# Seven products for sixteen instead of eight row chunks of each down projection

## The chip, the cores and the metric

One core of one Trainium2 chip runs the whole kernel. The metric is the device time of one launch in microseconds, the median of several runs.

## The reference, cut to what matters

A two-layer decoder trunk over 512 tokens of width 1024. Each layer has a gated feed-forward block, a mixer (attention and retention) and a second gated feed-forward block, each followed by a residual sum and a layer norm, so four feed-forward blocks run in all.

```python
D_MODEL = 1024; SEQ = 512; DEPTH = 2
D_FF = ((8 * D_MODEL // 3 + 127) // 128) * 128      # 2816, 22 chunks of 128

def swiglu_ffn(x, w_gu, w_down):
    a, u = jnp.split(x @ w_gu, 2, axis=-1)
    return (jax.nn.silu(a) * u) @ w_down

for l in range(DEPTH):
    x = layer_norm(DEEPNORM_ALPHA * x + 0.5 * swiglu_ffn(x, ffn1_w_gu[l], ffn1_w_down[l]), ...)
    x = layer_norm(DEEPNORM_ALPHA * x + hybrid_mixer(x, ...), ...)
    x = layer_norm(DEEPNORM_ALPHA * x + 0.5 * swiglu_ffn(x, ffn2_w_gu[l], ffn2_w_down[l]), ...)
```

The change is in the last matrix product of `swiglu_ffn`: a (512 x 2816) matrix of gated values times a (2816 x 1024) weight.

## The kernel before

**Every product in three matmuls.** All data are fp32. `split` (line 158) writes an operand as a rounded part on ScalarE (line 159, a cast) and a rest on VectorE (line 160, a subtraction that needs the cast). `mm3` (line 165) then issues three matmuls: high by high (line 168), high by low (169), low by high (170).

**Weights.** `Weights.pump` (line 50) walks a list of items, one for each unit of 128 x 1024 split weights, in the order in which TensorE uses them. There are six buffers for split units (`UBUFS`), and `W.done` frees one and starts the split of a later item into it. Raw weights come by SyncE's queue in pieces of 1 MB into two buffers (tag `raw`); the loads are started by `pump` ahead of their use.

**The gated half.** `ffn` (line 475) works through eleven pairs of chunks, the last nine by a seven-product scheme of their own (`glu7`), and leaves the gated values in `hT`: 22 chunks of 128 rows, 512 tokens wide. Its weight sums stand in two buffers of tag `S`.

**The down half.** Here `acc` is all eight PSUM banks: four blocks of 128 tokens (`t`) by two halves of 512 columns (`q`). Of the 22 chunks the first eight are taken as a 2 x 2 block product: `hT` is cut in two halves of four chunks and two halves of 256 tokens, the weight in two halves of 512 rows and two of 512 columns. Seven block products (`seventh`, line 680) replace eight. Each has two steps (`g`), and each step has 12 matmuls of 128 x 512 into two banks of one column half: `low`, `high`, `left`, `right` (lines 707 and 708). The other fourteen chunks take 24 matmuls each, into all eight banks (`chunk`, line 698; the last four, `TAIL`, by token block so that the norm of one block runs beside the next).

- Three of the seven products use weight blocks as they are (`p1`, `p2`, `p3` in `down_items`, line 340). The other four use sums of blocks, which are made in two SBUF tiles `R[0]` and `R[1]` (the two `S` buffers; each has two halves, `x` 0 and 1): SyncE loads a first block (line 356), and GpSimd adds others by accumulating DMAs (`add`, line 349). A sum that has been split may be added to again, for a later product (the third argument of `cut`).
- The token side needs sums too: `fifth` (three VectorE subtractions, lines 647 to 649) and `third` (one, line 655); the others are plain splits (`operand`, `whole`). A generator, `operands`, makes them three steps ahead, in four buffers.
- After some products `into` (line 710) adds the two banks to, or takes them from, the residual `Y` on VectorE (line 714). The next product that accumulates in those banks cannot write a bank until it has been read.

The order of the products before is: 1 `p1` into `low`, 2 sum into `high`, 3 `p2` into `left`, 4 sum into `low`, 5 `p3` into `right`, 6 sum into `low`, one plain chunk, 7 sum into `low`. Y is updated after 1, 2, 4 and 6. The order of instructions on each engine's queue is fixed when the program is built, by a list scheduler that follows program order and its own durations; each engine then runs its queue strictly in that order.

Of the kernel before, what the change touches and what calls it, by code (L numbers as in the profile page):

```python
# [7 lines left out]
F32 = mybir.dt.float32  # L8
F32R = mybir.dt.float32r
AF = mybir.ActivationFunctionType  # L10
ALU = mybir.AluOpType
# [7 lines left out]
P = 128  # L19
# [7 lines left out]
GN_EPS = 1e-6  # L27
SCALE = HD ** -0.5
TAIL = 4
SEVEN = (2, 3, 4, 5, 6, 7, 8, 9, 10)  # L30
UBUFS = 6
LOOK = 6
# [60 lines left out]
class Trunk:  # L93
# [230 lines left out]
    def ffn_items(self, gu, down, key):  # L324
        items = []
        for fp in range(NFP):
            a = self.cols_item(gu, fp * 256, (key, "a", fp))
            u = self.cols_item(gu, DFF + fp * 256, (key, "u", fp))
            if fp == 0:
                items += [a[0], u[0], a[1], u[1]]  # L330
            else:
                items += self.seven_items(a, u) if fp in SEVEN else a + u
        rows = []
        for fp in range(4, NFP):
            late = [self.tail_units if fp * 2 + c >= NF - TAIL else None for c in range(2)]
            rows += self.rows_item(down, fp * 256, (key, "d", fp), late)
        R = {}
        return items + self.down_items(down, key, R, rows[0]) + rows[1:]

    def down_items(self, w, key, R, row):  # L340

        def block(i, j, g):
            r0 = i * 512 + g * 256
            return w[r0 : r0 + 256, j * 512 : (j + 1) * 512].rearrange("(k p) c -> p k c", p=P)

        def add(g, x, i, j):
            self.tc.keep_in_program_order(self.nc.gpsimd.dma_start(R[g][:, x], block(i, j, g), accum_op=ALU.add))
# [22 lines left out]
        p1, p2, p3 = (self.wide_item(w, j * 512, i, (key, "b", i, j)) for i, j in ((0, 0), (1, 0), (1, 1)))  # L372
# [102 lines left out]
    def ffn(self, g_, b, out=None):  # L475
        nc, tc, W = self.nc, self.tc, self.W
        with ExitStack() as ctx:
# [99 lines left out]
            for fp in range(NFP):  # L577
                if fp == 0:
                    us = [W.get() for _ in range(6)]
                    self.pin = False  # L580
                    au = [us[0:2], us[2:4]]
                    self.finish(self.pend[:2])
                    more = []
                    for t0 in (0, 256):
                        for c in range(2):
                            glu(au[c], c, t0, t0 + 256)
                            if t0:
                                W.done(2)
# [41 lines left out]

            def part(g, i, j):

                return hT[:, j * 4 + 2 * g : j * 4 + 2 * g + 2, i * 256 : (i + 1) * 256]

            def operand(src):
                hh, hl = (v.rearrange("p (f t) -> p f t", f=2) for v in pair())
# [5 lines left out]
            def fifth(g):  # L642

                a11, a21, a22 = part(g, 0, 0), part(g, 1, 0), part(g, 1, 1)
                hh, hl = (v.rearrange("p (f t) -> p f t", f=2) for v in pair())
                s1 = self.s1[:, g]
                nc.vector.tensor_sub(s1, a21, a22)
# [13 lines left out]
                return hh, hl  # L661

            def operands():
                for g in range(2):
                    yield fifth(g)
                for g in range(2):
                    yield operand(part(g, 0, 1))
                for g in range(2):
                    yield operand(part(g, 0, 0))
                for g in range(2):  # L670
                    yield third(g)
                for g in range(2):
                    yield operand(part(g, 1, 0))
                yield whole(8)
                for g in range(2):
                    yield operand(part(g, 1, 1))
                for f in range(9, NF):
                    yield whole(f)

            def seventh(banks, u, h, new):  # L680

                for f in range(2):
                    for i, b_ in enumerate(banks):
                        ts = slice(i * P, (i + 1) * P)
                        self.mm3(b_, (h[0][:, f, ts], h[1][:, f, ts]), (u[0][:, f, :], u[1][:, f, :]),
                                 new and f == 0, False, skip_group_check=True)
                self.step()
# [25 lines left out]
                    y = self.Y[:, t0 + i, q * 512 : (q + 1) * 512]  # L713
                    nc.vector.scalar_tensor_tensor(out=y, in0=y, scalar=scale, in1=b_, op0=ALU.mult, op1=sign)

            for n, (banks, new, more) in enumerate((
                    (low, True, (0, 0, ALPHA)), (high, True, (0, 1, ALPHA)), (left, True, None),
                    (low, False, (0, 1, 1.0, ALU.subtract)), (right, True, None),
                    (low, False, (2, 1, ALPHA, ALU.subtract)), (low, False, None))):
                if n == 6:  # L720
                    chunk(8)
                for g in range(2):
                    u, h = W.get(), ahead.pop(0)
                    ahead.append(next(split))
                    seventh(banks, u, h, new and g == 0)
                    W.done(2 if n == 0 and g == 1 else 1)
                if more:
                    into(banks, *more)
# [400 lines left out]
```

## Time and profile before

| | |
|---|---|
| median of 3 runs | 1821.43 us (1821.35 to 1822.49) |
| the profiled execution: time / span | 1826.58 us / 1824.8 us |
| TensorE busy | 1800.6 us, 12074 matmuls |
| VectorE busy | 1339.8 us |
| ScalarE busy | 878.7 us |
| granted TensorE clock, mean | 0.995 |
| the down halves begin at | 234, 792, 1135 and 1695 us |

"Busy" counts overlapping pipelined matmuls once. PEclk is the granted TensorE clock as a share of full speed. In a timeline a row shows start, duration, engine, line, operation, output and inputs, count, and in brackets the idle time of the engine before it and what ended it. PE is TensorE, DVE VectorE, ACT ScalarE, POOL GpSimd, SP SyncE.

### The profile page before, as it was taken

The page shows a single profiled execution, that of the slowest core. Times are in us where ns is not written, and L with a number is a line of the kernel's source. Part 1 is how long each engine was busy: PE and PEld are TensorE (multiplying, and loading weights), DVE is VectorE, ACT ScalarE, POOL GpSimd, SP SyncE. Part 2 cuts the span into 40 slices and gives each one's busy share as a digit, 9 for nine tenths or more (in the row PEclk, how much of TensorE's full clock was granted, in tenths as well). Part 3 has the DMA queues.
Part 4 walks back from the last instruction along what each step waited for, and adds up shares of the span by engine and source line. Part 5 has one row for each costly group of instructions (what it writes and reads, how often), then busy time and mean ns, then how long its engine had stood idle before and what let it go on. Part 6 is the DMA issues. An engine that isn't in the chain of part 4 may idle for free.

```text
span 1824.8 us, 29291 instructions
## 1 busy us (share of the span) xinstructions
PE 1800.6 (99%) x12074; PEld 1632.9 (89%) x12074; DVE 1339.8 (73%) x1942; ACT 878.7 (48%) x1439; POOL 123.8 (7%) x104
## 2 busy tenths in 40 slices
PE   9999999999999999999999999999999999999998
PEld 9999978887789999988899999788877899999786
DVE  7888784656768788876678886847567687887845
ACT  4455553278723455554235554532785234555530
POOL 0000010111110000020000001001011100000101
PEclk9999999999999999999999999999999999999999
DMA  5233485223122332484222236641233122334731
GB/s 185 93 125 107 144 203 162 64 82 89 51 93 70 110 99 93 137 210 168 86 70 93 93 106 190 172 157 42 83 91 93 46 93 93 107 125 130 198 111 47
DMA packets 151990, 205.87 MB, mean 113 GB/s; under 512 B 4656, under 2 KB 116016, under 8 KB 151856
## 3 DMA queue, kind: packets, MB, share of 16 engines
q1 hardware_dynamic: 143152, 187.23, 31.5%
q0 software_dynamic: 8704, 16.78, 5.3%
q8 instruction: 94, 1.54, 0.4%
q14 instruction: 40, 0.33, 0.1%
HBM read 201.89 MB, written 2.10 MB: 112 GB/s over the span
## 4 chain that ended last, share of the span: by engine, by line
PE 82%; issue 7%; DVE 5%; ACT 3%; DMA 2%; POOL 1%; SPq 0%; POOLq 0%; DVEq 0%; ACTq 0%
PE ps L170 27%; PE ps L169 26%; PE ps L168 26%; DMA R<-in_ffn_w_down_dram 1%; ACT sw L898 1%; POOL sw L900 1%; PE ps L428 1%; DMA raw<-in_ffn_w_gu_dram 1%; DVE ul L160 1%; DVE Y L464 1%; ACT uh L159 1%; DVE st L454 1%; DVE Y L461 0%; PE ps L1008 0%; DVE Y L452 0%
## 5 line engine op out<-in xcount | busy, mean ns | idle before, releaser
L168 PE MATMUL ps<-xh,uh 128*128 128x256 f32 (+1 forms) x1616 | 482.1, 298 | 0.0
L170 PE MATMUL ps<-xh,ul 128*128 128x256 f32 (+1 forms) x1616 | 479.1, 297 | 0.4 <-DVE ul L160 0.4
L169 PE MATMUL ps<-xl,uh 128*128 128x256 f32 (+1 forms) x1616 | 478.8, 296 | 0.4 <-DVE xl L160 0.4
L160 DVE TENSOR_TENSOR ul<-raw,uh 128x1024 fp32r<-128x1024 f32 (+1 forms) x325 | 336.6, 1049 | 77.9 <-ACT uh L159 77.2
L159 ACT CAST uh<-raw 128x1024 fp32r<-128x1024 f32 (+1 forms) x325 | 291.4, 913 | 202.9 <-PE ps L169 127.6
L168 PE MATMUL ps<-Th,uh 128*128 128x256 f32 x1152 | 319.3, 277 | 0.7 <-DVE Q L547 0.7
L169 PE MATMUL ps<-Tl,uh 128*128 128x256 f32 x1152 | 318.7, 277 | 0.0
L170 PE MATMUL ps<-Th,ul 128*128 128x256 f32 x1152 | 318.3, 276 | 0.0
L168 PEld LDWEIGHTS ps<-xh,uh 128*128 128x128 f32 x1616 | 307.9, 191 | 10.2 <-issue 1.6
L170 PEld LDWEIGHTS ps<-xh,ul 128*128 128x128 f32 x1616 | 307.9, 191 | 9.3 <-DVE ul L160 0.8
L169 PEld LDWEIGHTS ps<-xl,uh 128*128 128x128 f32 x1616 | 308.0, 191 | 8.6 <-DVE xl L160 0.8
L170 PE MATMUL ps<-uh,hl 128*128 128x512 f32 x640 | 255.0, 398 | 4.0 <-DVE hl L160 4.0
L168 PE MATMUL ps<-uh,hh 128*128 128x512 f32 x640 | 253.4, 396 | 4.7 <-ACT hh L159 4.7
L169 PE MATMUL ps<-ul,hh 128*128 128x512 f32 x640 | 253.6, 396 | 0.0
L159 ACT CAST uh<-S 128x1024 fp32r<-128x1024 f32 x144 | 151.2, 1050 | 153.1 <-PE ps L169 148.2
L160 DVE TENSOR_TENSOR ul<-S,uh 128x1024 fp32r<-128x1024 f32 x144 | 175.9, 1222 | 62.1 <-ACT uh L159 61.4
L168 PEld LDWEIGHTS ps<-Th,uh 128*128 128x128 f32 x1152 | 216.7, 188 | 0.9 <-DVE Q L547 0.9
L169 PEld LDWEIGHTS ps<-Tl,uh 128*128 128x128 f32 x1152 | 216.7, 188 | 0.0
L170 PEld LDWEIGHTS ps<-Th,ul 128*128 128x128 f32 x1152 | 216.4, 188 | 0.0
L168 PEld LDWEIGHTS ps<-uh,hh 128*128 128x128 f32 x640 | 121.7, 190 | 33.2 <-ACT hh L159 6.4
L170 PEld LDWEIGHTS ps<-uh,hl 128*128 128x128 f32 x640 | 122.0, 191 | 31.9 <-DVE hl L160 6.4
L169 PEld LDWEIGHTS ps<-ul,hh 128*128 128x128 f32 x640 | 121.9, 190 | 27.7
(141 smaller groups left out, 2247.8 us busy)
## 6 DMA issues: line engine op xcount, KB each, us to landing
raw<-in_ffn_w_gu_dram SPq DMA_DIRECT2D x86, 1024.0 KB, 5.5
raw<-in_ffn_w_down_dram SPq DMA_DIRECT2D x40, 1024.0 KB, 5.0
raw<-in_w_in_dram SPq DMA_DIRECT2D x18, 1024.0 KB, 5.4
R<-in_ffn_w_down_dram POOLq DMA_DIRECT2D x32, 512.0 KB, 7.6
R<-in_ffn_w_down_dram SPq DMA_DIRECT2D x16, 512.0 KB, 5.2
raw<-in_w_in_dram SPq DMA_DIRECT2D x8, 512.0 KB, 4.6
raw<-in_w_out_dram SPq DMA_DIRECT2D x8, 512.0 KB, 6.1
raw<-in_w_out_dram SPq DMA_DIRECT2D x4, 1024.0 KB, 4.9
```

Of the source, the lines that this page charges most:

```text
L159: a = self.nc.scalar.copy(hi, src)
L160: b = self.nc.vector.tensor_sub(lo, src, hi.bitcast(F32))
L168: mm(out, ah, bh, start=start, stop=False, **kw)
L169: mm(out, ah, bl, start=False, stop=False, **kw)
L170: mm(out, al, bh, start=False, stop=stop, **kw)
L428: nc.tensor.transpose(b[:, c * P : (c + 1) * P], src[:, c * P : (c + 1) * P], self.ident)
L454: nc.vector.bn_stats(out=st[:, h, :], in_=y[:, hs])
L464: nc.vector.scalar_tensor_tensor(out=y[:, hs], in0=y[:, hs], scalar=rs, in1=b[:, hs], op0=ALU.mult, op1=ALU.add)
L898: nc.scalar.copy(sw[q * 32 : q * 32 + 32, :n], src[o * 32 : o * 32 + 32, :n])
L900: nc.gpsimd.tensor_mul(sw[:, :n], sw[:, :n], S)
```

## The change

Sixteen chunks instead of eight go by seven products, in two runs of eight chunks (`RUNS = 2`). Six plain chunks are left, the last four as before. Within a run the order of the products changes: 1 `p2` into `left`, 2 `p1` into `low`, 3 sum into `high`, 4 `p3` into `right`, 5, 6 and 7 sums into `low`, with no plain chunk between them. Sums for products 3, 5 and 7 stand in half 0 of `R`, each made out of the one before as soon as that one has been split; product 6 uses half 1. The second run loads `R` anew when the first has split it for the last time. `seventh` now goes through its two banks one after the other (six matmuls in a row into a bank) instead of through the chunks. Y is updated after products 2, 3, 5 and 6 of each run, and between the runs twice more, for `low` and `high`; so the last norm no longer scales Y. The operand that is split ahead of the stage is that of the new first product (chunks 4 to 7 instead of 0 to 3). The load of the norm's weights (`load_ln`) into an `S` buffer moves from chunk 12 to chunk 16.

```diff
+RUNS = 2
...
-        rows = []
-        for fp in range(4, NFP):
+        R = {}
+        for n in range(RUNS):
+            items += self.down_items(down, (key, n), R, n)
+        for fp in range(4 * RUNS, NFP):
...
-            r0 = i * 512 + g * 256
+            r0 = run * 1024 + i * 512 + g * 256
...
-                    R[g] = self.spool.tile([P, 2, 2, 512], F32, tag="S", name=self.nm("R"), bufs=2)
+                    if run == 0:
+                        R[g] = self.spool.tile([P, 2, 2, 512], F32, tag="S", name=self.nm("R"), bufs=2)
...
-        p1[0] = p1[0][:3] + (begin(p1[0][3]),)
-        return (p1 + [cut(g, 0, (0, 1, 1)) for g in range(2)] + p2
-                + [cut(g, 0, (0, 1, 0)) for g in range(2)] + p3 + [cut(g, 1) for g in range(2)]
-                + [row] + [cut(g, 0) for g in range(2)])
+        p2[0] = p2[0][:3] + (begin(p2[0][3]),)
+        return (p2 + p1 + [cut(g, 0, (0, 1, 1)) for g in range(2)] + p3
+                + [cut(g, 0, (0, 1, 0)) for g in range(2)] + [cut(g, 1) for g in range(2)]
+                + [cut(g, 0) for g in range(2)])
...
-                    self.split(*(v.rearrange("p g f t -> p (g f) t") for v in hv), hT[:, 0:4, :256])
+                    self.split(*(v.rearrange("p g f t -> p (g f) t") for v in hv), hT[:, 4:8, :256])
...
             def operands():
-                for g in range(2):
-                    yield fifth(g)
-                for g in range(2):
-                    yield operand(part(g, 0, 1))
...
-                yield whole(8)
...
-                for f in range(9, NF):
+                for n in range(RUNS):
+                    gs = range(2 * n, 2 * n + 2)
+                    if n:
+                        for g in gs:
+                            yield operand(part(g, 0, 1))
+                    for g in gs:
+                        yield operand(part(g, 0, 0))
+                    for g in gs:
+                        yield fifth(g)
+                    for g in gs:
+                        yield third(g)
+                    for i, j in ((0, 0), (1, 0), (1, 1)):
+                        for g in gs:
+                            yield operand(part(g, i, j))
+                for f in range(8 * RUNS, NF):
                     yield whole(f)
...
-                for f in range(2):
-                    for i, b_ in enumerate(banks):
-                        ts = slice(i * P, (i + 1) * P)
+                for i, b_ in enumerate(banks):
+                    ts = slice(i * P, (i + 1) * P)
+                    for f in range(2):
...
+            for n in range(RUNS):
+                scale = 1.0 if n else ALPHA
+                for banks, new, more in (
+                        (left, n == 0, None), (low, True, (0, 0, scale)), (high, True, (0, 1, scale)),
+                        (right, n == 0, None), (low, False, (0, 1, 1.0, ALU.subtract)),
+                        (low, False, (2, 1, scale, ALU.subtract)), (low, False, None)):
+                    for g in range(2):
+                        u, h = W.get(), ahead.pop(0)
+                        ahead.append(next(split))
+                        seventh(banks, u, h, new and g == 0)
+                        W.done(2 if first and g else 1)
+                    first = False
+                    if more:
+                        into(banks, *more)
+                if n < RUNS - 1:
+                    into(low, 2, 0, scale)
+                    into(high, 2, 1, 1.0)
-            for f in range(9, NF - TAIL):
-                if f == 12:
+            for f in range(8 * RUNS, NF - TAIL):
+                if f == 8 * RUNS:
                     gb = self.load_ln(self.spool, g_, b, "S", 2)
...
-                self.norm(t, acc[t], gb, out, DELAY[t], (1.0 if t < 2 else ALPHA, 1.0))
+                self.norm(t, acc[t], gb, out, DELAY[t], (1.0 if t < 2 or RUNS > 1 else ALPHA, 1.0))
```

More of the change, by code (lines that the diff above doesn't have):

```diff
@@ L332, in ffn_items, with down_items @@
                 items += self.seven_items(a, u) if fp in SEVEN else a + u
-        rows = []
-        for fp in range(4, NFP):
+        R = {}
+        for n in range(RUNS):
+            items += self.down_items(down, (key, n), R, n)
+        for fp in range(4 * RUNS, NFP):
             late = [self.tail_units if fp * 2 + c >= NF - TAIL else None for c in range(2)]
[L336 to L340, printed above, removed]
+            items += self.rows_item(down, fp * 256, (key, "d", fp), late)
+        return items
+    def down_items(self, w, key, R, run):
         def block(i, j, g):
-            r0 = i * 512 + g * 256
+            r0 = run * 1024 + i * 512 + g * 256
             return w[r0 : r0 + 256, j * 512 : (j + 1) * 512].rearrange("(k p) c -> p k c", p=P)
@@ L370, in cut @@
             return (None, None, None, go)
-        p1, p2, p3 = (self.wide_item(w, j * 512, i, (key, "b", i, j)) for i, j in ((0, 0), (1, 0), (1, 1)))
-        p1[0] = p1[0][:3] + (begin(p1[0][3]),)
-        return (p1 + [cut(g, 0, (0, 1, 1)) for g in range(2)] + p2
-                + [cut(g, 0, (0, 1, 0)) for g in range(2)] + p3 + [cut(g, 1) for g in range(2)]
-                + [row] + [cut(g, 0) for g in range(2)])
+        p1, p2, p3 = (self.wide_item(w, j * 512, 2 * run + i, (key, "b", i, j)) for i, j in ((0, 0), (1, 0), (1, 1)))
+        p2[0] = p2[0][:3] + (begin(p2[0][3]),)
+        return (p2 + p1 + [cut(g, 0, (0, 1, 1)) for g in range(2)] + p3
+                + [cut(g, 0, (0, 1, 0)) for g in range(2)] + [cut(g, 1) for g in range(2)]
+                + [cut(g, 0) for g in range(2)])
     def mix_items(self, w_in, w_out, key):
@@ L631, in part @@
             def part(g, i, j):
-                return hT[:, j * 4 + 2 * g : j * 4 + 2 * g + 2, i * 256 : (i + 1) * 256]
+                f = g // 2 * 8 + j * 4 + g % 2 * 2
+                return hT[:, f : f + 2, i * 256 : (i + 1) * 256]
             def operand(src):
@@ L645, in fifth @@
                 hh, hl = (v.rearrange("p (f t) -> p f t", f=2) for v in pair())
-                s1 = self.s1[:, g]
+                s1 = self.s1[:, g % 2]
                 nc.vector.tensor_sub(s1, a21, a22)
@@ L714, in into @@
                     nc.vector.scalar_tensor_tensor(out=y, in0=y, scalar=scale, in1=b_, op0=ALU.mult, op1=sign)
[L716 to L728, printed above, removed]
-            for f in range(9, NF - TAIL):
-                if f == 12:
+            first = True
+            for n in range(RUNS):
[17 more added lines that the diff above has]
+                if f == 8 * RUNS:
                     gb = self.load_ln(self.spool, g_, b, "S", 2)
```

8 lines of the change are left out of this document (removed).

## The prediction

> **What bounds the kernel now.** I read the page first: busy times, then the chain that ended last.
>
> ```profile
> span 1824.8 us, 29291 instructions
> PE 1800.6 (99%) x12074; PEld 1632.9 (89%) x12074; DVE 1339.8 (73%) x1942; ACT 878.7 (48%) x1439; POOL 123.8 (7%) x104
> PE 82%; issue 7%; DVE 5%; ACT 3%; DMA 2%; POOL 1%; SPq 0%; POOLq 0%; DVEq 0%; ACTq 0%
> ```
>
> TensorE is never long without work, and the chain is TensorE for 82%: fewer matmuls shorten the kernel where nothing else ends the stage. Next, windows over TensorE: a quiet stretch of the first down half, then the first 18 us of all four.
>
> ```profile
> 250.00:268.00 18.00, 18.00 (x80) 1.00 0.66 175
> 250.00:330.00 80.00, 80.00 (x351) 1.00 0.52 158
> ...
> 234.00:252.00 18.00, 16.05 (x64) 0.91 0.95 205
> 792.40:810.40 18.00, 16.47 (x70) 1.00 1.00 209
> 1134.80:1152.80 18.00, 15.63 (x61) 0.91 1.00 202
> 1695.00:1713.00 18.00, 15.18 (x54) 0.81 0.94 193
> ```
>
> 351 matmuls in 80 us are 0.228 us each, 2.74 us for a step of 12. The quiet 18 us hold 80; the four openings hold 64, 70, 61 and 54, that is 71 too few, or 71 x 0.228 = 16.2 us lost, in three of them with the granted clock down too. The TensorE timeline of the first opening shows where:
>
> ```profile
> 233.96 0.39 PE L168 MATMUL ps<-uh,uh 128*128 128x512 f32 x1
> ...
> 239.19 0.39 PE L170 MATMUL ps<-uh,ul 128*128 128x512 f32 x1
> 240.65 0.50 PE L168 MATMUL ps<-uh,hh 128*128 128x512 f32 x1 [1.07 <-ACT hh L159]
> 240.99 0.40 PE L169 MATMUL ps<-ul,hh 128*128 128x512 f32 x1
> 242.26 0.51 PE L170 MATMUL ps<-uh,hl 128*128 128x512 f32 x1 [0.88 <-DVE hl L160]
> ...
> 243.41 0.63 PE L170 MATMUL ps<-uh,hl 128*128 128x512 f32 x1
> 243.84 0.63 PE L168 MATMUL ps<-uh,hh 128*128 128x512 f32 x1
> ...
> 245.97 0.44 PE L170 MATMUL ps<-uh,hl 128*128 128x512 f32 x1
> ```
>
> The stage begins at 233.96; times "in" count from there. Product 2 waits for its token sum, 1.07 us for the cast and 0.88 us for the rest; then matmuls come every 0.43 us until 246. ScalarE, VectorE, GpSimd and the chain say why:
>
> ```profile
> 236.50 1.05 ACT L159 CAST uh<-R 128x1024 fp32r<-128x1024 f32 x1 [4.93 <-DMA R<-in_ffn_w_down_dram]
> 237.58 1.23 DVE L160 TENSOR_TENSOR ul<-R,uh 128x1024 fp32r<-128x1024 f32 x1 [3.58 <-ACT uh L159]
> 239.18 0.69 DVE L647 TENSOR_TENSOR s<-hT 128x512 f32<-128x512 f32 x1
> ```
> ```profile
> 221.62 4.22 DMA R<-in_ffn_w_down_dram
> 226.39 10.01 DMA R<-in_ffn_w_down_dram
> ```
> ```profile
> 226.39 2.44 POOL L349 DMA_DIRECT2D R<-in_ffn_w_down_dram  x2 [3.88 <-DMA R<-in_ffn_w_down_dram]
> 236.66 1.21 POOL L349 DMA_DIRECT2D R<-in_ffn_w_down_dram  x1 [5.22 <-DMA R<-in_ffn_w_down_dram]
> 239.52 1.20 POOL L349 DMA_DIRECT2D R<-in_ffn_w_down_dram  x1 [1.65 <-DVE hT L563]
> ```
>
> The accumulating DMA takes 10.01 us; VectorE's in-order queue stands 3.58 us on its split, and the token subtraction (239.18) is behind it. Then VectorE is the full engine, by its own timeline and a window from all engines:
>
> ```profile
> 249.22 1.28 DVE L714 SCALAR_TENSOR_TENSOR Y<-Y,ps 128x512 f32<-128x512 f32 x2
> 250.42 0.69 DVE L160 TENSOR_TENSOR hl<-hT,hh 128x512 fp32r<-128x512 f32 x1
> 251.02 1.22 DVE L160 TENSOR_TENSOR ul<-raw,uh 128x1024 fp32r<-128x1024 f32 x1
> 252.16 0.68 DVE L160 TENSOR_TENSOR hl<-hT,hh 128x512 fp32r<-128x512 f32 x1
> ```
> ```profile
> 239.20:275.20 36.00, 34.05 (x141) 27.21 (x140) 34.25 (x44) 20.75 (x27) 3.63 (x3) 0.95 0.70 181
> ```
>
> Start to start, a Y update or operand split costs VectorE 0.60 us and a weight split 1.14. It is busy 34.25 of 36 us (third column) while products go at full rate.
>
> **The change part by part.**
>
> *Fewer matmuls.* A run is 14 x 12 = 168 matmuls for 8 x 24 = 192: 24 less in each of four blocks, 96 x 0.228 = 21.9 us gained, on the path.
>
> *The opening.* Products 1 and 2 now use raw weights, and product 2 a plain operand. The first sum is due at 2 x 5.48 = 11 us into the stage; it was split at 237.58, 3.6 us in. I count all 16.2 us as gained (bounds 8, if half of it stays because product 2's operand is still late, and 16.2).
>
> *VectorE's ledger.* From the opening to the Y update after product 5 of run 1 its queue holds 11 weight splits (12.5 us), 11 operand splits (6.6), eight sums on the token side (4.8), four Y updates (2.4) and a last gate product (0.4): 26.7 us. Product 5 ends at 10 x 2.74 = 27.4. There was a plain chunk or another bank pair between these products; now VectorE has no slack in 27 us, so each wait of its queue is paid.
>
> *The waits.* The adds for product 5 can start when the splits for product 3 are done. Those need buffers freed at 0 and 2.7 us, as the adds at 236.66 and 239.52 did, 2.7 and 5.6 in. They took:
>
> ```profile
> R<-in_ffn_w_down_dram POOLq DMA_DIRECT2D x2, 512.0 KB, 7.6
> ```
> ```profile
> 244.57 9.80 SPq L265 DMA_DIRECT2D raw<-in_ffn_w_down_dram  x2
> ```
> ```profile
> 215.00:220.00 5.00, 5.00 (x44) 5.00 (x44) 2.87 (x4) 2.50 (x4) 0.00 (x0) 1.00 0.89 302
> ```
>
> So they land at 10.3 and 13.2. New is a raw load of 1 MB for run 2, which starts when `p1` is split, at about -1; the next such load was issued at 244.57, 10.6 us in. At 302 GB/s it needs 3.5 us of the DMA engines. I put the landings at 11.3 and 16.5 (bounds 10.3 and 13.2 without collision; 13.8 and 18 with all of it ahead). VectorE has emptied its list before the first of these splits at 0.3 + 0.4 + 4 x 1.14 + 10 x 0.60 = 11.3, and before the second 1.14 + 0.60 after the first's cast, at 14.1: with ScalarE's cast (1.05) it waits 1.0 and 3.5 us. The cast of product 4's operand is behind the second on ScalarE, ready at 18.2 for 16.4, and its rest at 19.6: TensorE waits 2.7 us (bounds 0 and 5).
>
> *Product 5 to 6 and 6 to 7.* Both use `low`, so bank 0 must be read within the 6 x 0.228 = 1.37 us in which product 5 fills bank 1. VectorE's update would be done at 0.3 + 26.7 + 4.5 + 0.7 = 32.2, TensorE ready at 27.4 + 2.7 + 1.9 (clock, below) = 32.0. But the four first subtractions of run 2's token sums depend on nothing late and can stand ahead of it: 2.4 us more, a wait of 2.6 (bounds 0 and 5). From 6 to 7, a weight split in flight and the read, 1.14 + 0.69, overrun the cover by 0.5, with an operand split ahead by 1.1; I take 1.0 in each run (bounds 0 and 1.5).
>
> *Clock.* The opening lost 9 matmuls x (0.43 - 0.228) = 1.8 us after some 2 us of idling, in the fourth block (54 matmuls, clock 0.81) more. Two spells of 1.9 for the waits of product 4 and 6: 3.8 (bounds 0 and 6).
>
> *Costing nothing.* Run 2's first sums: reload and add took 4.22 + 10.01 us; from the last split of run 1 (some 27 us) they are in by 43 and due at 49; if that cover goes, each microsecond late is paid. On SyncE the loads of `R` wait for those splits, with run 2's third raw load behind them, due at 55. GpSimd's queue holds only adds here, in the order of use. The load of the norm's weights moves behind run 2's last splits, 25 us before the norm:
>
> ```profile
> ln<-in_ln_b_dram SPq DMA_DIRECT2D x6, 512.0 KB, 4.9
> ```
>
> Uncovered it would cost 4.9 us a block. The Y updates between the runs are needed 5 us later. In run 2 VectorE has 14 x 1.74 + 8 x 1.2 = 34 us of work for 38. The norm's scale and the early split keep their shapes.
>
> *Sum.* A block loses 2.7 + 2.6 + 2.0 + 3.8 = 11.1 us, four 44.4. Net -21.9 - 16.2 + 44.4 = +6.3. The profiled execution (1826.6, span 1824.8) would give 1832.9; it stands 5.2 over the median, so 1821.4 + 6.3 = 1828.
>
> **The rivals.** The balance is at a loss of 38.1 / 4 = 9.5 us a block.
>
> *VectorE keeps up (faster).* If the adds land by 10.3 and 13.2, VectorE waits 0 and 0.2 us, the update after product 5 is on time and only the handover 6 to 7 is left, with 1 us for 5 to 6 and 1 of clock: 4 us a block, -22, 1799 us. For it: six matmuls a bank give 1.37 us of cover, and before, VectorE ran 36 us full without holding up TensorE. Against it: the 10.01 us add beside a raw load. The Trainium skill, "DMA: Bandwidth & Descriptors", section "Anatomy of one DMA — SWDGE (gpsimd) path", gives 2.0 us plus bytes over 436 GB/s, an estimate of 3.2 us for such an add, which would land them sooner still; the trace, at 7.6 and 10.01, does not agree.
>
> *The waits stay at full clock (faster).* If no wait is long enough in one piece to bring the clock down, a block loses 7.3: 29.2 - 38.1 = -9, 1812. For it: the second opening had no drop (1.00), with 10 matmuls lost. Against: the three others. The Trainium skill, "TensorE: Matmul & The Clock Gate", section "Part 1: The HAM clock gate (the "warmup" mystery)", halves the clock after an idle window of about 3.4 us; by that rule waits of 2.7 and 2.6 us would stay at full clock. The trace does not agree: 1.07 and 0.88 us with two matmuls between were followed by matmuls at 0.43.
>
> *Sums late in run 2 (slower).* If each add of run 1 is late by 3 us more, the reload slips past 49 us and run 2 pays again: 15 us a block, 60 - 38.1 = +22, 1843.
>
> **Numbers.** Forecast 0.45 (in it 0.20 within, 0.25 above), VectorE keeps up 0.22, full clock 0.15, late sums 0.18. Within 0.2% (3.6 us) is about what a measurement of this kernel can tell from no change. Of the forecast the part with a block's loss of 8.6 to 10.4 is "the same". Faster 0.37, the same 0.20, slower 0.43. Range 1799 to 1842; the forecast's own 1820 to 1838.
>
> **What would show it.** In the profile after: 11,978 matmuls; openings with 80 matmuls in 18 us; then TensorE waiting for ScalarE's `hh` or VectorE's `hl` at product 4, for line 714's successor before products 6 and 7 of run 1, the clock under 1 there; VectorE's gaps released by the casts of `R`. It is wrong if VectorE has no gap before 30 us, if those Y updates start within 1 us of their matmul, or if run 2 shows new waits for `R`.

## The result, and the profile after

The changed kernel takes 1833.26 us (median of 5 runs, 1831.67 to 1838.21), the kernel before 1822.49 on the same chip: a ratio of 1.006, with a 95% interval of 1.0042 to 1.0077. It is slower by 10.8 us, where 6.3 were forecast. The profiled executions (1826.58 and 1832.97) differ by 6.4, because that of the kernel before stood 4.1 us over its median. That the forecast came so near is partly luck, as the section on the prediction shows.

The page of the changed kernel, span, busy times and the chain that ended last:

```profile
span 1830.9 us, 29442 instructions
PE 1785.7 (98%) x11978; PEld 1616.3 (88%) x11978; DVE 1427.6 (78%) x2070; ACT 916.1 (50%) x1487; POOL 163.0 (9%) x136
PE 70%; DVE 10%; issue 8%; DMA 7%; ACT 4%; POOL 2%; SPq 0%; POOLq 0%; DVEq 0%; ACTq 0%
```

TensorE has 96 matmuls fewer, but its share of the chain falls from 82% to 70%: VectorE goes from 5% to 10%, DMA from 2% to 7%. Windows over TensorE of the first 13.7 us of each down half show that the opening is cured:

```profile
233.46:247.16 13.70, 13.70 (x62) 1.00 1.10 236
794.45:808.15 13.70, 13.70 (x62) 1.00 1.10 238
1139.98:1153.68 13.70, 13.70 (x62) 1.00 1.10 259
1701.45:1715.15 13.70, 13.70 (x62) 1.00 1.10 241
```

No stage loses anything there. The losses come right behind it. The list of what TensorE waited for (us in total, times, longest) and, from its timeline, the waits of the first block:

```profile
PE ps L169 <- DVE Y L720: 15.5, 8, 3.2
PE ps L171 <- DVE hl L161: 8.6, 9, 1.5
PE ps L169 <- ACT hh L160: 5.5, 4, 2.2
```
```profile
248.95 0.51 PE L169 MATMUL ps<-uh,hh 128*128 128x512 f32 x1 [1.64 <-ACT hh L160]
250.90 0.51 PE L171 MATMUL ps<-uh,hl 128*128 128x512 f32 x1 [1.21 <-DVE hl L161]
...
259.01 0.50 PE L171 MATMUL ps<-uh,hl 128*128 128x512 f32 x1 [0.75 <-DVE hl L161]
...
267.71 0.47 PE L169 MATMUL ps<-uh,hh 128*128 128x512 f32 x1 [0.64 <-DVE Y L720]
...
309.97 0.77 PE L169 MATMUL ps<-uh,hh 128*128 128x512 f32 x1 [3.23 <-DVE Y L720]
```

In order these rows are the second step of product 3 (its operand, cast and rest), the second step of product 4, product 6 of run 1 and product 6 of run 2. What stood in the way of the first two is on ScalarE's and VectorE's timelines:

```profile
247.34 1.04 ACT L160 CAST uh<-R 128x1024 fp32r<-128x1024 f32 x1 [6.45 <-PE ps L171]
248.29 0.61 ACT L160 CAST hh<-s 128x512 fp32r<-128x512 f32 x1
```
```profile
242.35 0.68 DVE L652 TENSOR_TENSOR s<-hT 128x512 f32<-128x512 f32 x1
248.41 1.23 DVE L161 TENSOR_TENSOR ul<-R,uh 128x1024 fp32r<-128x1024 f32 x1 [5.38 <-ACT uh L160]
249.56 0.69 DVE L653 TENSOR_TENSOR hT<-hT 128x512 f32<-128x512 f32 x1
250.16 0.68 DVE L161 TENSOR_TENSOR hl<-s,hh 128x512 fp32r<-128x512 f32 x1
```

The sum `s` for product 3's second operand was ready at 243.0. Its cast (`hh<-s`) stands on ScalarE behind the first split for product 5 (`uh<-R`), which waits for an add. (The row names TensorE, whose last matmul ended just then, at 247.32; with plain DMAs the same cast starts at 241.01, so it is the add that it waited for.) VectorE stands idle for 5.38 us on the same split with the operand's rest (`hl<-s`) queued behind. Product 5 begins 21.9 us into the stage; its weights were waited for at 14. The add had taken, by DMA issues in two windows of one microsecond (from 236 and from 240):

```profile
R<-in_ffn_w_down_dram POOLq DMA_DIRECT2D x1, 512.0 KB, 10.9
R<-in_ffn_w_down_dram POOLq DMA_DIRECT2D x1, 512.0 KB, 11.2
```

They were issued at 236.38 and 240.08 and landed at 247.26 and 251.31. In run 2, TensorE waits longest for the Y update after product 5. VectorE is busy all the time there, with other work ahead of it:

```profile
305.13 1.22 DVE L161 TENSOR_TENSOR ul<-R,uh 128x1024 fp32r<-128x1024 f32 x1
306.27 1.22 DVE L161 TENSOR_TENSOR ul<-raw,uh 128x1024 fp32r<-128x1024 f32 x1
307.40 0.69 DVE L161 TENSOR_TENSOR hl<-hT,hh 128x512 fp32r<-128x512 f32 x1
308.00 1.22 DVE L161 TENSOR_TENSOR ul<-raw,uh 128x1024 fp32r<-128x1024 f32 x1
309.14 1.28 DVE L720 SCALAR_TENSOR_TENSOR Y<-Y,ps 128x512 f32<-128x512 f32 x2
```

The split at 308.00 is for the first plain chunk, the one at 306.27 for the last four chunks, which begin at 333.

For the rest I use one number for each kernel, the **loss**: in the four down halves, the time from each matmul's start to the next one's, summed over what is beyond the pace of 0.229 us, without 5.3 us at the norms that all kernels have. Before it is 17.2 us, after 46.5: 11.6 us a block, of which some 5.8 at products 3 and 4 of run 1, 0.9 at product 6 of run 1, 4.6 at product 6 of run 2 and 0.4 at product 4 of run 2. Some 46 matmuls at 0.427 us behind such waits are in it (46 x 0.198 = 9.1 us). 46.5 - 17.2 - 21.9 = +7.4 us, for spans of 1830.9 and 1824.8. Single waits of TensorE in the text below are counted the same way, from start to start beyond the pace: the row with 3.23 us of idle time is a wait of 3.40.

### The profile page after: what moved, and what is told of

The parts are those of the page before. It is cut to its first block, busy times and chain, and to the rows that moved or that the text cites. A ratio compares the mean times of both kernels' runs of the same rounds, so it can differ in the third digit from the quotient of the medians.

```text
span 1830.9 us, 29442 instructions
## 1 busy us (share of the span) xinstructions
PE 1785.7 (98%) x11978; PEld 1616.3 (88%) x11978; DVE 1427.6 (78%) x2070; ACT 916.1 (50%) x1487; POOL 163.0 (9%) x136
## 3 DMA queue, kind: packets, MB, share of 16 engines
q8 instruction: 94, 1.54, 0.4%
## 4 chain that ended last, share of the span: by engine, by line
PE 70%; DVE 10%; issue 8%; DMA 7%; ACT 4%; POOL 2%; SPq 0%; POOLq 0%; DVEq 0%; ACTq 0%
PE ps L169 22%; PE ps L171 22%; PE ps L170 22%; DMA R<-in_ffn_w_down_dram 6%; DVE ul L161 3%; DVE hl L161 1%; ACT sw L909 1%; POOL R L351 1%; ACT uh L160 1%; DMA raw<-in_ffn_w_gu_dram 1%; DVE Y L467 1%; PE ps L431 1%; DVE st L457 1%; DVE Y L720 1%; DVE Y L464 1%
## 5 line engine op out<-in xcount | busy, mean ns | idle before, releaser
L160 ACT CAST uh<-raw 128x1024 fp32r<-128x1024 f32 (+1 forms) x317 | 282.5, 910 | 221.3 <-PE ps L170 146.2
L161 DVE TENSOR_TENSOR ul<-raw,uh 128x1024 fp32r<-128x1024 f32 (+1 forms) x317 | 326.7, 1046 | 63.4 <-ACT uh L160 62.5
L169 PE MATMUL ps<-uh,hh 128*128 128x512 f32 x608 | 244.5, 402 | 20.9 <-DVE Y L720 15.5
L171 PE MATMUL ps<-uh,hl 128*128 128x512 f32 x608 | 244.2, 402 | 8.6 <-DVE hl L161 8.6
L170 PE MATMUL ps<-ul,hh 128*128 128x512 f32 x608 | 242.2, 398 | 0.0
L351 POOL DMA_DIRECT2D R<-in_ffn_w_down_dram x64 | 77.9, 1317 | 1050.7 <-DMA R<-in_ffn_w_down_dram 484.5
L169 PEld LDWEIGHTS ps<-uh,hh 128*128 128x128 f32 x608 | 116.9, 192 | 50.4 <-issue 14.5
L171 PEld LDWEIGHTS ps<-uh,hl 128*128 128x128 f32 x608 | 116.8, 192 | 39.6 <-DVE hl L161 14.3
```

The costliest lines, as they stand in the source:

```text
L160: a = self.nc.scalar.copy(hi, src)
L161: b = self.nc.vector.tensor_sub(lo, src, hi.bitcast(F32))
L169: mm(out, ah, bh, start=start, stop=False, **kw)
L170: mm(out, ah, bl, start=False, stop=False, **kw)
L171: mm(out, al, bh, start=False, stop=stop, **kw)
```

## The experiments

All are compared with the kernel before, on the same chip as its runs. Ratios have 95% intervals.

| kernel | us | ratio to before | loss, us |
|---|---|---|---|
| before | 1821.8 | 1 | 17.2 |
| changed | 1833.3 | 1.006 [1.0042, 1.0077] | 46.5 |
| plain DMAs | 1794.3 | 0.9849 [0.9835, 0.9864] | 9.1 |
| splits of R behind operands | 1833.7 | 1.0068 [1.0054, 1.0081] | 50.3 |
| Y update first | 1823.9 | 1.0015 [1.0007, 1.0023] | 40.7 |
| one run | 1837.1 | 1.0087 [1.0072, 1.0102] | 29.4 |
| adds in order | 1841.2 | 1.0106 [1.0092, 1.012] | 56.1 |
| adds in order, Y first | 1843.1 | 1.0114 [1.01, 1.0128] | 57.8 |
| adds in order, loop by chunk | 1842.8 | 1.0112 [1.0098, 1.0126] | 59.2 |
| adds in order, one run | 1834.8 | 1.0065 [1.0051, 1.0078] | 27.8 |
| splits 4 ahead | 1817.2 | 0.997 [0.996, 0.9979] | 30.5 |
| splits 4 ahead, Y first | 1807.2 | 0.9915 [0.99, 0.9929] | 21.3 |
| the same, adds in order | 1818.1 | 0.9969 [0.9957, 0.9981] | 31.5 |
| splits 4 ahead, Y first, rows pinned | 1795.1 | 0.9851 [0.9838, 0.9865] | 5.7 |

**Is it the late sums?** GpSimd's DMAs write and do not add, so this kernel leaves out the additions that make the sums.

```diff
-self.nc.gpsimd.dma_start(R[g][:, x], block(i, j, g), accum_op=ALU.add)
+self.nc.gpsimd.dma_start(R[g][:, x], block(i, j, g))
```

> GpSimd's DMAs into R write instead of adding (the sums of weight blocks are left out; every queue has the same instructions in the same order). Theory of the late sums: a plain 512 KB DMA lands in 5 to 6 us instead of 10.9 and 11.2, product 5's splits stop waiting, and the waits at products 3 and 4 of run 1 vanish: 20 us and their slow matmuls less, about 1812. If bytes and not the addition set the time (collision with the raw load), they land as late as before and the time stays at 1833. The 3.40 us before product 6 of run 2 depend on no DMA by the theory of the queue order and stay (within 0.3 us).

Measured: 39 us less than the changed kernel, twice what was expected. The page's median from issue to landing and the list of TensorE's waits, with plain DMAs:

```profile
R<-in_ffn_w_down_dram POOLq DMA_DIRECT2D x64, 512.0 KB, 4.8
```
```profile
PE ps L169 <- DVE Y L720: 5.6, 8, 0.8
```

In the changed kernel the median is 8.6. The waits at products 3 and 4 are gone, and the wait before product 6 of run 2 fell too, from 3.40 to 0.93 us, though no DMA is among the instructions ahead of it: VectorE had stood 2.28 us on a late sum some 18 us earlier and was still behind. So my sentence that this wait depends on no DMA was wrong. The 0.80 us at product 6 of run 1 stays to the hundredth, and with the sums in time sixteen chunks by seven products are worth 27.5 us over before.

**Only the place of the splits that wait.** The splits of R keep the place in the queue that the program gives them.

```diff
-    def split(self, hi, lo, src):
+    def split(self, hi, lo, src, pin=False):
...
-        if self.pin:
+        if self.pin or pin:
...
-                self.split(hv, lv, R[g][:, x])
+                self.split(hv, lv, R[g][:, x], True)
```

> Only the place of the splits of R in the two queues changes: each stays behind the operand split that the program puts ahead of it, on ScalarE and VectorE. Theory of the queue order: the waits at the second step of product 3 (1.4 to 3.5 us in each block) and the slow matmuls behind them vanish, since its operand now stands ahead of the split that waits for the sum. The second sum, landing some 17.9 us into the stage, then still stands ahead of `third`'s second addition, so product 4 may wait up to 4 us in its second step: net 0 to 3 us a block, 1821 to 1833. Theory of the late sums alone (whoever waits, the time of the landing decides): the wait at product 3 stays at 1.4 us or more, no change in time. Rival, a full VectorE: the same loss a block, only moved, within 1 us of 26.5 us in all. The wait of 3.40 us before product 6 of run 2 stays in all theories.

Measured: the wait at product 3 is gone in all four blocks, and TensorE waits 2.7 to 3.6 us at product 4 instead. The loss is 50.3 us; in run 2 the wait before product 6 is 3.8 us in three blocks and 2.3 in one. The timelines of TensorE and VectorE:

```profile
257.21 0.50 PE L169 MATMUL ps<-uh,hh 128*128 128x512 f32 x1 [3.41 <-ACT hh L160]
```
```profile
253.43 1.22 DVE L161 TENSOR_TENSOR ul<-R,uh 128x1024 fp32r<-128x1024 f32 x1 [2.24 <-ACT uh L160]
254.57 1.28 DVE L720 SCALAR_TENSOR_TENSOR Y<-Y,ps 128x512 f32<-128x512 f32 x2
255.77 0.69 DVE L660 TENSOR_TENSOR hT<-hT 128x512 f32<-128x512 f32 x1
```

`third`'s second addition (L660) is now the one behind a waiting split, the second of product 5. The waits went as the theory of the queue order said, and the time is 0.7 us over the upper end of its range. By the size alone a full VectorE would have said the same: the first runs lose 25.9 us for 26.5. This run does not decide between the two.

**The order of the adds.** The adds for product 6 were ahead of those for product 5 in GpSimd's queue, and the queue is served one add after the other: landings at 235.80, 239.82, 243.86 (the last two for product 6), 247.26 and 251.31.

```diff
-                for g in range(2):
-                    add(g, 1, 1, 1)
                 return go(v, hi, lo)
...
                 for a in after:
-                    add(g, *a)
+                    add(*a)
...
-        return (p2 + p1 + [cut(g, 0, (0, 1, 1)) for g in range(2)] + p3
-                + [cut(g, 0, (0, 1, 0)) for g in range(2)] + [cut(g, 1) for g in range(2)]
+        late = [(0, 1, 1, 1), (1, 1, 1, 1)]
+        return (p2 + p1 + [cut(g, 0, (g, 0, 1, 1), *late[:2 * g]) for g in range(2)] + p3
+                + [cut(g, 0, (g, 0, 1, 0)) for g in range(2)] + [cut(g, 1) for g in range(2)]
```

> GpSimd's adds are queued in the order in which their sums are used: the two adds for product 6 (the other halves of R) are issued behind the two for product 5 instead of ahead of them. Every queue keeps as many instructions of the same kind in the same order. Theory of the add queue: its adds are served one after the other, 3.4 to 4.0 us each while a raw load runs (in the changed kernel they land at 235.80, 239.82, 243.86, 247.26 and 251.31), so the sums for product 5 land at some 7 and 11 us into the stage instead of 13.8 and 17.9, no split stands on them, the waits at products 3 and 4 vanish and the 3.40 us before product 6 of run 2 fall to about the 0.93 of the kernel with plain DMAs: 1795 to 1800. Rival: an add beside a raw load takes 10 us by itself, whatever stands ahead; then the sums land 12 us into the stage or later and the time stays over 1823.

Measured: the sums for product 5 do land early, by DMA issues in the two windows from 236 and 239:

```profile
R<-in_ffn_w_down_dram POOLq DMA_DIRECT2D x1, 512.0 KB, 5.7
R<-in_ffn_w_down_dram POOLq DMA_DIRECT2D x1, 512.0 KB, 6.0
```

The wait at product 3 is gone. But the time rises to 1841. VectorE's timeline says why:

```profile
250.94 1.23 DVE L161 TENSOR_TENSOR ul<-R,uh 128x1024 fp32r<-128x1024 f32 x1 [0.43 <-ACT uh L160]
255.04 1.23 DVE L161 TENSOR_TENSOR ul<-R,uh 128x1024 fp32r<-128x1024 f32 x1 [2.88 <-ACT uh L160]
256.18 1.29 DVE L161 TENSOR_TENSOR hl<-hT,hh 128x512 fp32r<-128x512 f32 x2
```

Product 6's second sum now lands at 253.87, 20.3 us into the stage for a use at 30.2, and its split stands ahead of the operands for product 4 (`hl` at 256.18). So the rule is not "sums in the order of use": whichever sum comes late, its split stands six steps ahead of use, and what is due first is behind it. Of my two theories the one on the service of the queue held and its forecast of the time failed.

**One run**, in the changed kernel and with the adds in order.

```diff
-RUNS = 2
+RUNS = 1
```

> One run of the new order instead of two (RUNS = 1), so 12,074 matmuls, as many as before. In the changed kernel TensorE loses 26.5 us in the first runs of the four blocks and 20.0 in the second ones; before, the down halves lost 17.2. If the losses of the first run belong to the order of the products (sums for product 5 that stand ahead in the queues of ScalarE and VectorE), they stay: before + 26.5 - 17.2 = + 9, some 1832 us. Rival, crowding by the second run (its raw load, its early token subtractions): the first run then loses under 10 us in all, and the time is 1815 or less.

> The adds in order of use, one run instead of two (12,074 matmuls). If the sixteen chunks keep up with TensorE once the sums are in time, the second run is worth its 96 matmuls (21.9 us) less some 1 us of handover a block: this kernel is 17 to 19 us over the adds in order with two runs, and under before by what its opening lost (17 us) less some 1 us a block. If the second run costs VectorE time that TensorE then waits for, the difference is under 12 us.

Measured: 1837.1 where some 1832 were expected, with a loss of 29.4 us in the one run; in the changed kernel the first runs lose 26.5. So the wait comes with the new order of products and not with the second run. The second run gains 3.8 us here (21.9 us of matmuls for 17.1 us more loss). With the adds in order it costs 6.3 us: the 17 to 19 us gain of that expectation is not there, since with two runs the loss is 28.3 us larger.

**The Y update's place.** The update is put ahead of the splits that the freed buffers start. In the first kernel this is done after products 5 and 6 (the two whose `more` has four entries; the expectation names product 5 alone), and both buffers of the product are given back behind the update:

```diff
-                        W.done(2 if first and g else 1)
+                        if len(more or ()) < 4:
+                            W.done(2 if first and g else 1)
...
+                    if len(more or ()) == 4:
+                        self.pin = True
+                        W.done(2)
+                        self.pin = False
```

In the second kernel, which has the adds in order, it is done after each product that updates Y, and only the second buffer waits for the update:

```diff
                         seventh(banks, u, h, new and g == 0)
-                        W.done(2 if first and g else 1)
+                        if not g or more is None:
+                            W.done(2 if first and g else 1)
                     first = False
                     if more:
                         into(banks, *more)
+                        self.pin = True
+                        W.done()
+                        self.pin = False
```

> Only around product 5: the Y update is put in the queue before the weights' buffers of product 5 are given back, and the weight splits that this starts stay behind it. Theory of the queue order: the 3.40 us before product 6 of run 2 fall under 1 us and the 0.80 in run 1 under 0.4, with the slow matmuls after the former gone in three blocks (some 1.6 us each): 4 x 3 + 5 = 17 us less, 1816. Theory of a full VectorE: the splits put off are missing later, waits before product 7 or the plain chunk of at least 2 us a block appear, gain under 8 us. The waits at products 3 and 4 of run 1 stay.

> The adds in order of use, and after every product that updates Y the update is put in the queue before the second step's weight buffer is given back; the split that this starts stays behind it. If the 0.80 us before product 6 of run 1 and the 0.9 of run 2 are the order of VectorE's queue, they fall under 0.3 and nothing comes back: 6 us less than with the adds in order alone. If VectorE is full, the splits put off come back as waits of 0.5 us or more in run 2 (as at products 3 of run 2 with the update first alone), and the time is the same within 3 us.

Measured: 9.4 us less than the changed kernel, about half of what the order theory said. At product 6 run 1's 0.80 vanishes and run 2's 3.40 becomes 1.54; 0.7 to 1.0 us at one or two places of run 2's product 4 are new (the second expectation calls it product 3). With the adds in order nothing is gained: the time is the same within 3 us, as the expectation of a full VectorE had it, but by another way. 5.2 to 6.3 us of wait appear at product 6 of run 1, where the update stands behind the second split for product 7 and that split stands 3.33 us on its sum. Moving the update alone treats one instruction of a queue whose order is wrong in other places.

**The loop over the banks**, back to chunk by chunk, with the adds in order.

```diff
-                for i, b_ in enumerate(banks):
-                    ts = slice(i * P, (i + 1) * P)
-                    for f in range(2):
+                for f in range(2):
+                    for i, b_ in enumerate(banks):
+                        ts = slice(i * P, (i + 1) * P)
```

> The adds in order of use, and the two banks of a product taken chunk by chunk again instead of bank by bank: the first bank is then complete 3 matmuls (0.7 us) before the end of a product, not 6 (1.37 us), and the second bank is wanted after 3. If the six matmuls a bank cover the read of the banks, each of the handovers 5 to 6 and 6 to 7 costs 0.7 to 1.4 us more, in two runs of four blocks: 11 to 22 us over the adds in order alone. If the Y update is late by its place in VectorE's queue, whatever the cover, the difference is under 4 us.

Measured: the interval overlaps that of the adds in order. The waits before product 6 are 0.80 us in run 1 and 3.89 in run 2 with either loop: the update is late by its place in the queue, whatever the cover. What the cover is worth in a kernel without these waits was not tried.

**Splits nearer to use.** Four steps ahead instead of six, the splits of R pinned as above:

```diff
-        while self.emitted < len(self.items) and self.emitted < self.taken + LOOK:
+        while self.emitted < len(self.items) and self.emitted < self.taken + self.look:
...
+                        W.look = LOOK if first and not g else 4
                         W.done(2 if first and g else 1)
...
+            W.look = LOOK
```

The last line stands behind the two runs.

> Weights are split four steps ahead of use instead of six while the two runs last, and the splits of R stay behind the operand splits that the program puts ahead of them; the adds are queued as in the changed kernel. In the changed kernel the sums for product 5 land 13.8 and 17.9 us into the stage and are wanted at 21.9 and 24.7; only their splits, put in the queues 14 and 16 us ahead of use, stood on them. Theory of splits too far ahead in queues that run in order: the waits at products 3 and 4 of run 1 (22.9 us and their slow matmuls) vanish and are not found elsewhere but for up to 3 us a block before product 6, where the split for product 7 stands ahead of the Y update; run 2 has no backlog, its 3.40 us fall under 1.5: 1800 to 1812. Rival, the sums themselves (or VectorE) have no time for two runs: the waits move to products 5 to 7 and the loss stays over 35 us in all, 1822 or more.

> As the splits four steps ahead, and the Y update is put in the queue before the second step's weight buffer is given back. Theory of the queue order: the waits before product 6 fall under 0.5 us in both runs, 4 to 12 us less than without it: 1794 to 1803. Rival, a full VectorE: what it gains there comes back at products 1 to 3 of run 2, within 3 us of the other.

> Adds in order of use, splits four steps ahead, Y update first. With the adds in order alone the sums for product 5 landed 8.6 and 11.9 us into the stage and those for product 6 at 16.2 and 20.3; their splits now come at 13.7, 16.4, 19.2 and 21.9, so none stands on a sum before product 7. Theory of the splits too far ahead: 1792 to 1800, as the kernel with plain DMAs, and within 3 us of the kernel with the adds as they were, since there too the sums land ahead of use. Rival, the service of the add queue (8 adds of some 4 us in a run of 38 us): the adds for product 7 and for run 2 come later by being behind product 6's, new waits at product 7 or product 3 of run 2, over 1805.

Measured: without the update first, 1817.2, over the range given; all waits at products 3 and 4 are gone, and what is left is mostly the Y update at product 6 (2.0 to 3.6 us in run 1, 1.1 to 4.6 in run 2). With the update first 1807.2, also over its range: run 1 has a wait before product 6 in one block only (0.93), but run 2 keeps 2.2 to 3.2 us there. With the adds in order as well 1818.1, with 4.1 to 5.1 us at product 6 of run 2. That is over 1805, as its rival said, but at none of the products that the rival named, and 11 us from the kernel with the adds as they were, where the theory said 3. Both had left out the following. VectorE's timeline of the kernel at 1807.2, ahead of product 6 of run 2 (line numbers are one higher in these kernels):

```profile
298.46 1.22 DVE L162 TENSOR_TENSOR ul<-raw,uh 128x1024 fp32r<-128x1024 f32 x1
299.60 0.69 DVE L162 TENSOR_TENSOR hl<-hT,hh 128x512 fp32r<-128x512 f32 x1
300.20 1.28 DVE L721 SCALAR_TENSOR_TENSOR Y<-Y,ps 128x512 f32<-128x512 f32 x2
```

The split at 298.46 and one at 294.45 are for the last four chunks, which begin some 25 to 30 us later; nothing pinned them, and the planner of the queues had put them here. With the adds in order such a split costs more, as ScalarE's timeline of that kernel shows:

```profile
295.53 1.05 ACT L161 CAST uh<-raw 128x1024 fp32r<-128x1024 f32 x1 [4.98 <-DMA raw<-in_ffn_w_down_dram]
```

The cast for the last four chunks stands 4.98 us on its raw load, VectorE 4.41 us behind it, and the update starts only at 303.49. So the same fault can occur without any sum; no run takes this one split away from that kernel. The last experiment pins them:

```diff
-                self.split(hi, lo, v[:, c, :])
+                self.split(hi, lo, v[:, c, :], key[1] == "d")
```

> As the kernel with splits four steps ahead and the Y update first; besides, the splits of the plain chunks' weights stay behind what the program puts ahead of them. There (run 2) two splits for the last four chunks, wanted 40 us later, stand among those for products 6 and 7 ahead of the Y update (294.45 and 298.46 in the first block; the update starts at 300.20, and TensorE waits 2.2 to 3.2 us for it before product 6 in the four blocks, some 1 us more at product 7 in three). Theory of the queue order: without these two splits (2 x 1.14 us) the update comes some 2.3 us earlier, the wait before product 6 falls under 1 us and the one at product 7 under 0.5: 9 to 13 us less, 1794 to 1799. Rival, VectorE is full: the splits put off are late in the tail, where waits of 1 us or more at the plain chunks appear, and the time stays over 1803.

Measured: 1795.1, the ratio to before 0.9851 [0.9838, 0.9865], 38 us under the changed kernel. The page, TensorE's waits for the Y update, and the windows over all engines of the first block's two runs (TensorE, its loads, VectorE, ScalarE, GpSimd):

```profile
span 1789.7 us, 29408 instructions
R<-in_ffn_w_down_dram POOLq DMA_DIRECT2D x64, 512.0 KB, 9.0
```
```profile
PE ps L170 <- DVE Y L721: 3.8, 4, 1.4
```
```profile
232.87:271.37 38.50, 38.50 (x171) 31.57 (x170) 37.71 (x51) 22.53 (x29) 8.55 (x8) 1.00 0.96 220
271.37:309.87 38.50, 37.06 (x163) 30.11 (x162) 32.82 (x43) 21.41 (x28) 6.01 (x5) 1.00 0.84 200
```

The adds still take 9.0 us, and in the first block the sums for product 5 land 13.0 and 15.5 us into the stage, for 13.8 and 17.9. The kernel has the time of the one with plain DMAs without a faster DMA: in run 1 nothing that is due soon stands behind a sum any more. And there VectorE is busy 37.71 of 38.50 us while TensorE never waits. So neither the service of the add queue nor VectorE's capacity forces the loss of the changed kernel; both rivals fall, as far as two runs of this shape go. The loss took both, late sums and work queued behind them, and taking away either one leaves 5.7 to 9.1 us of it. What remains, 5.7 us, is mostly the wait before product 6 of run 2 (0.7 to 1.6 us). In the first block, where it is longest, VectorE still stands 0.45 us on a late sum just ahead of that update; what makes up the rest was not tried.

## Why the prediction was right, and where it was not

The sign was right, and the size within a factor of two: 6.3 us forecast, 10.8 measured. Step by step:

- *Fewer matmuls, the opening*: right, 11,978 matmuls and 62 of them in each first 13.7 us. "80 matmuls in 18 us" did not come, since the new wait begins some 13.7 us into the stage.
- *VectorE's ledger*: right. The kernel with the rows pinned shows 37.71 of 38.50 us busy. "Each wait of its queue is paid" held roughly: in run 1 of the first block VectorE stood 5.8 us on late sums and TensorE waited 4.9.
- *The waits*: the mechanism was right (the queue stands on splits of sums for product 5, an operand is behind) and two steps under it failed. First, "GpSimd's queue holds only adds here, in the order of use": product 6's two adds are ahead of product 5's, and the sums landed 13.8 and 17.9 us into the stage, at the upper bounds given (13.8 and 18) and not at 11.3 and 16.5. That they met these bounds is luck: the bounds put the whole raw load ahead, and with the adds in order, beside the same raw loads, the sums landed 8.6 and 11.9 us in. Second, the ledger put all operands of product 3 ahead of the first such split; in the queue the last one is behind it. So TensorE stops a product earlier than said, and waits 4.5 us a block at products 3 and 4 where 2.7 were forecast.
- *Product 5 to 6 in run 1*: 0.9 us for 2.6. The subtractions that "can stand ahead" of the update stand behind it in the queue, and TensorE, late by some 6 us, gave VectorE that time.
- *Product 6 to 7*: nothing for 1.0 in each run.
- *Clock*: 2.3 us a block for 3.8. In the first block a window from 251 to 255 us, right behind the waits at product 3, shows a granted clock of 0.57.
- *Costing nothing in run 2*: this failed, and by the mark that the prediction itself set ("new waits for `R`"). VectorE has "34 us of work for 38" there, but a sum says nothing of the order: its sums were late as well, and splits wanted long after stood ahead of the update. 4.0 us a block, without the clock.
- *Sum*: 11.1 us a block were forecast and 11.6 lost. The 1.8 and 4.0 us that were missing and the 1.7, 2.0 and 1.5 that were too many cancel.

The rivals: "the waits stay at full clock" fell, and "sums late in run 2" came in part: it put a block's loss at 15 us, and run 2 does pay again, but 4 us. "VectorE keeps up" gave 1799; the kernel with plain DMAs (1794) shows that its condition, sums in time, was rightly named, and the one at 1795 that its condition was too narrow: a late sum is harmless if nothing due is queued behind its split.

The Trainium skill, "Perfetto Trace Analysis", section "Tensor Engine Instruction (MATMUL, LD_WEIGHTS)", calls the queues of ScalarE, VectorE and GpSimd strictly first in, first out. The trace agrees: 5.38 us of standing with a ready subtraction (249.56) behind.

## What to carry to other kernels

Read a queue that runs in order by the due time of what stands behind a waiting instruction, not by the landing of what it waits for: the same slow transfers cost 1833 us with the weights prepared six steps ahead, and 1795 with them prepared four steps ahead and behind what is due sooner (median from issue to landing 8.6 and 9.0 us). A sum of an engine's work against the time available says whether a schedule exists, not whether the order in the queue is one. When a wait is removed by making one transfer earlier, see which transfer that makes later: the adds "in order of use" cost 8 us here.

## What the runs showed of the hardware

- Issue on GpSimd (ns, min/median/max), in the changed kernel and with plain DMAs:

```profile
L351 POOL DMA_DIRECT2D R<-in_ffn_w_down_dram x64: 1194/1212/2242, 221.0 to 1762.6; - x64
```
```profile
L351 POOL DMA_DIRECT2D R<-in_ffn_w_down_dram x64: 722/722/872, 220.3 to 1725.8; - x64
```

  An accumulating DMA of 512 KB takes GpSimd 1212 ns and a plain one 722, in the same place of the same queue; the medians from issue to landing are 8.6 and 4.8 us. In the first block of the changed kernel the queued accumulating DMAs landed 3.4 to 4.1 us after each other, beside raw loads. The medians of the raw loads of 1 MB are 8.2 and 6.1 us in these two kernels; but with the rows pinned it is 6.4, beside adds that are as slow, so the adds alone do not set it.
- Half pace does not follow from the length of a wait. Before product 6 of run 2 the wait is 3.40 us in all four blocks, and 5, 0, 7 and 8 slow matmuls follow; waits of 0.96 and 1.38 us at product 3 were followed by 8 in the second block, and waits of 0.95 and 1.38 by none in the fourth. The Trainium skill, "TensorE: Matmul & The Clock Gate", section "Part 1: The HAM clock gate (the "warmup" mystery)", says that the window in which activity is counted runs freely, so that the number of slow matmuls at a kernel's start varies with its phase. The different counts behind equal waits would fit that, if it holds behind a wait too, which no run here tests; its figure of about 3.4 us of idling does not cover the waits of 0.96 and 1.38 us.
